# A fourth of the weight splits: low part from an accumulating DMA instead of a VectorE subtraction

## The chip, the cores and the metric

The kernel runs on one core of one Trainium2 chip. The metric is the device time of one execution in microseconds (us); less is better. Two executions of the kernel before are given, and one execution under the hardware profiler, from which all views below come. The engines are TensorE (PE, with its weight loads shown apart as PEld), VectorE (DVE), ScalarE (ACT), GpSimd (POOL) and SyncE (SP), and 16 DMA engines that move data between HBM and the on-chip memory.

## What is computed

A two-layer decoder trunk for 256 tokens of width 2048, in float32. Layer 0 has stick-breaking attention, layer 1 has differential attention over keys and values of its own; each layer ends in a squared-ReLU MLP of width 8192. What matters here is that nearly all the work is products of activations with weight matrices, each of which is read from HBM once:

```python
qkv = (x @ w_qkv)                  # 2048 x 6144
...
h = merge_blocks(o) @ w_o          # 2048 x 2048
x = layer_norm(DEEPNORM_ALPHA * x + h, ...)
h = jax.nn.relu(x @ w_up)          # 2048 x 8192
x = layer_norm(DEEPNORM_ALPHA * x + (h * h) @ w_down, ...)
...                                # layer 1: kv = x @ w_kv (2048 x 4096), q = x @ w_q, o @ w_o, MLP
```

## The kernel before

**Split operands.** TensorE multiplies in a format with fewer significant bits than float32 (fp32r). The kernel therefore writes every operand as a sum of a high and a low part and forms three products, high by high, high by low and low by high, in one accumulator. The function `split` makes the parts: ScalarE copies the source into the narrow format, which gives the high part (line 58), and VectorE subtracts that from the source, which gives the low part (line 61).

**Pieces of weights.** `wchunk` delivers the weights in 768 pieces of 128 partitions by 1024 elements, 512 KB each, in the order in which the matmuls use them: 96 for the queries, keys and values of layer 0, 32 for its output projection, 256 for its MLP, then 96, 32 and 256 for layer 1. In this text piece 388, for instance, is the 388th of them. A piece is loaded into a staging tile `st` (4 buffers; the load is issued by SyncE at line 67), its high part goes to `wh` and its low part to `wl` (7 buffers each). So no more than seven pieces are split at a time, and a piece's high part can be written only when the matmuls of the piece seven before it are done.

**Loops.** `by_token` computes 512 output columns for all tokens (one accumulator for each half of the tokens, 12 matmuls a piece; the first call of a phase takes the pieces in runs of two). `by_column` computes the transposed product (four accumulators, 16 matmuls a piece). `out_proj` and the second half of `mlp` use the activations as weights of TensorE and share each activation tile between two pieces. In `mlp`'s second half, blocks of 24 matmuls use two pieces in turn: the first two accumulators of a half of the tokens take the first piece, the other two the second. All matmuls are recorded at line 148 (function `mm`).

**Between phases.** At the end of `out_proj` and `mlp` the function `residual` adds a finished accumulator to `xs` on VectorE, and `layernorm` normalizes 128 tokens: `mv` and `ve` (lines 132 and 134) on VectorE, the inverse root `rstd` on GpSimd (line 136), the scaling of four slices on VectorE (lines 140 and 141), and then four transposes on TensorE (line 90), split again into `xT` (lines 58 and 61). The next phase begins with `by_token`, which uses the first half of the tokens while the second is still being normalized.

**Order.** The code writes down dependencies only; a scheduler at build time fixes the order of the instructions on each engine. Each engine then works through its own list in that order and waits on semaphores. GpSimd had 20 instructions in all: four initial ones, eight `rstd` and eight `rr`, the same kind of inverse root inside the attention of layer 1 (line 490).

The functions that the change touches follow, with the line numbers of the profile.

Of the kernel before, what the change touches and what calls it, by code (L numbers as in the profile page):

```python
# [10 lines left out]
AF = mybir.ActivationFunctionType  # L11
ALU = mybir.AluOpType
AX = mybir.AxisListType

P = 128
# [12 lines left out]
LAMBDA_INIT = 0.8 - 0.6 * math.exp(-0.3 * 1)  # L28
CH = 1024
RUN = 2  # L30
ST_BUFS = 4
W_BUFS = 7

# [2 lines left out]
def trunk(ctx: ExitStack, tc: tile.TileContext, x, ln_g, ln_b, sb_w_qkv, sb_w_o, kv_w, diff_w_q,  # L36
          diff_lambda, diff_subln_g, diff_w_o, mlp_w_up, mlp_w_down, consts, rope, out):
    nc = tc.nc
# [4 lines left out]
    wp = ctx.enter_context(tc.tile_pool(name="wp", bufs=W_BUFS))  # L43
    ps = ctx.enter_context(tc.tile_pool(name="ps", bufs=1, space=bass.MemoryType.PSUM))

    uid = [0]

    def nm(s):
        uid[0] += 1
# [3 lines left out]
        return ps.tile([P, 512], F32, tag=tag, name=nm(tag), bufs=5 if tag == "acc" else 3)  # L53

    def split(hi, lo, src, hi_engine=None):
        """src (float32) = hi + lo exactly, each with at most 12 significant bits."""
        if hi_engine is None:
            nc.scalar.activation(hi, src, AF.Copy)  # L58
        else:
            hi_engine.tensor_copy(hi, src)  # L60
        nc.vector.tensor_tensor(lo, src, hi.bitcast(F32), op=ALU.subtract)  # L61

    def wchunk(src):
        """A [P, a, b] piece of a weight matrix, a * b = CH, as its two parts."""
        a, b = src.shape[1], src.shape[2]
        st = wp.tile([P, CH], F32, tag="st", bufs=ST_BUFS, name=nm("st"))
        nc.sync.dma_start(st.rearrange("p (a b) -> p a b", a=a), src)
        hi = wp.tile([P, CH], F32R, tag="wh", name=nm("wh"))
        lo = wp.tile([P, CH], F32R, tag="wl", name=nm("wl"))
        split(hi, lo, st)  # L70
        return hi.rearrange("p (a b) -> p a b", a=a), lo.rearrange("p (a b) -> p a b", a=a)

# [1 line left out]
    nc.scalar.preload_act_table_set("natural_log_exp_and_others")  # L74
    xs = base.tile([P, NT, D], F32, name="xs")
    xT = base.tile([P, KT, 2, T], F32R, name="xT")
# [7 lines left out]
    nc.vector.memset(neghalf, -0.5)  # L84

    def transposed(t, j, src):
        """src [P tokens, 512] -> its part of xT."""
        pt = acc("at")
        for i in range(4):
            nc.tensor.transpose(pt[:, i * P:(i + 1) * P], src[:, i * P:(i + 1) * P], ident)  # L90
        hi = xT[:, 4 * j:4 * j + 4, 0, t * P:(t + 1) * P]
        lo = xT[:, 4 * j:4 * j + 4, 1, t * P:(t + 1) * P]
        split(hi, lo, pt.rearrange("p (a b) -> p a b", a=4))
# [6 lines left out]
    background = []  # L100

    def tick():
        """Emit the next step of attention between two chunks of a projection."""
        if background:
            step = background.pop(0)
            if step:
                step()

    def load_gb(layer, i, allocate, after):
        """The norm's weights and biases on all partitions, in four pieces. The loads wait for  # L110
        `after`, so that they take no space before the phase that uses them."""
        pieces = []
        for j in range(4):
            sl = slice(j * 512, (j + 1) * 512)
            g, b = allocate(j)
            for piece, src in ((g, ln_g), (b, ln_b)):
                nc.vector.tensor_copy(piece[:, 0:1], after)
                nc.scalar.dma_start(piece, src[layer, i:i + 1, sl].broadcast_to((P, 512)))
            pieces.append((g, b))
        return pieces  # L120
# [27 lines left out]
        nc.tensor.matmul(o, l, r, start=start, stop=stop)  # L148

    def by_token(w, n0, staggered=False, between=None):  # L150
        """[tokens, 512 columns] of x @ w: one accumulator for each half of the tokens."""
        accs = [acc() for _ in range(NT)]
        run = RUN if staggered else 1
        for c0 in range(0, KT // 2, run):
            chunks = [
                wchunk(w[2 * c * P:(2 * c + 2) * P, n0:n0 + 512].rearrange("(a p) n -> p a n", p=P))
                for c in range(c0, c0 + run)
            ]
            for t in range(NT):
                ts = slice(t * P, (t + 1) * P)  # L160
                if between and c0 == 0 and t == 1:
                    between()
                for c, (wh, wl) in zip(range(c0, c0 + run), chunks):
                    for kk in range(2):
                        k = 2 * c + kk
                        mm(accs[t], xT[:, k, 0, ts], wh[:, kk, :], k == 0, False)
                        mm(accs[t], xT[:, k, 0, ts], wl[:, kk, :], False, False)
                        mm(accs[t], xT[:, k, 1, ts], wh[:, kk, :], False, k == KT - 1)
            tick()
        return accs  # L170

    def by_column(w, n0):
        """(x @ w).T for 512 columns: four accumulators [128 columns, 2, tokens], whose two
        halves are to be added."""
        accs = [acc() for _ in range(4)]
        for c in range(KT // 2):
            wh, wl = wchunk(w[2 * c * P:(2 * c + 2) * P, n0:n0 + 512].rearrange("(a p) n -> p a n", p=P))
            for f in range(4):
                fs = slice(f * P, (f + 1) * P)
                for kk in range(2):  # L180
                    k = 2 * c + kk
                    if k == 0:
                        mm(accs[f], wh[:, kk, fs], xT[:, k, :, :], True, False)
                        mm(accs[f][:, :T], wl[:, kk, fs], xT[:, k, 0, :], False, False)
                    else:
                        mm(accs[f][:, :T], wl[:, kk, fs], xT[:, k, 0, :], False, False)
                        mm(accs[f], wh[:, kk, fs], xT[:, k, :, :], False, k == KT - 1)
            tick()
        return accs

    def folded(pool, psum, scale=1.0):
        """The sum of an accumulator's halves, times scale."""
        b = pool.tile([P, T], F32, tag="evb", bufs=2, name=nm("evb"))
        nc.scalar.activation(b, psum[:, T:], AF.Copy, scale=scale)  # L194
        s = pool.tile([P, T], F32, tag="evs", bufs=2, name=nm("evs"))
        if scale == 1.0:
            nc.vector.tensor_tensor(s, psum[:, :T], b, op=ALU.add)  # L197
        else:
            nc.vector.scalar_tensor_tensor(s, psum[:, :T], scale, b, op0=ALU.mult, op1=ALU.add)
        return s  # L200
# [12 lines left out]
        return vs  # L213

    def gb_pieces(pool):
        """Space for the norm's weights and biases where queries and keys were."""
        return lambda j: [pool.tile([P, 512], F32, tag=tag, bufs=4, name=nm("gb")) for tag in "qk"]

    def out_proj(w, oT, gb_of):
        """x = norm(alpha * x + o @ w)"""  # L220
        stats = new_stats()
        lag = 4
        for nh in range(2):
# [5 lines left out]
            for ks in sets:  # L229
# [5 lines left out]
                else:  # L235
                    chunks = {}
# [69 lines left out]
                    if ks[-1] == FT - 1:  # L306
                        layernorm(t, stats[t], gb, last)

# [1 line left out]
    with tc.tile_pool(name="sb", bufs=1) as pool:  # L310
        oT = pool.tile([P, KT, 2, T], F32R, name="oTa")
        w = sb_w_qkv[0]
# [2 lines left out]
        sps = [pool.tile([P, 2, 512], F32R, name=f"sp{i}") for i in range(2)]  # L315
        aps = [pool.tile([P, 2, 512], F32R, name=f"ap{i}") for i in range(2)]

        # Scores lie as [keys, queries]: [later keys, all queries | earlier keys, all queries].
        # The first P columns (later keys, earlier queries) are masked whole and held at zero.
        live, tris = slice(P, 512), slice(P, P + T)  # L320
        blocks = ((1, slice(0, T)), (0, slice(T, 512)))

        def attend(h, q, k, vs):
            """The steps of one head."""
            i = h % 4
            sh, sl = sps[i % 2][:, 0, :], sps[i % 2][:, 1, :]
            ah, al = aps[i % 2][:, 0, :], aps[i % 2][:, 1, :]
# [66 lines left out]
        out_proj(sb_w_o[0], oT, lambda: load_gb(0, 0, gb_pieces(pool), oT[:, KT - 1, 0, 0:1].bitcast(F32)))  # L394
    mlp(0, False)

# [1 line left out]
    with tc.tile_pool(name="df", bufs=1) as pool:  # L398
        oT = pool.tile([P, KT, 2, T], F32R, name="oTb")
        tri = pool.tile([P, T], F32, name="trib")  # L400
# [32 lines left out]
            nc.vector.tensor_tensor(s[0:32, :], s[0:32, :], r, op=ALU.add)  # L433
            return parts(pool, tag, s)

        # Scores lie as [queries, keys]: [later queries, all keys | earlier queries, earlier keys].
        rows = ((1, slice(0, T)), (0, slice(T, 384)))
        tris = slice(P, P + T)

        def attend2(h, qs, ks, vs):  # L440
            """The steps of one head."""
            wT = pool.tile([P, 2, 384], F32R, tag="wT", bufs=2, name=nm("wT"))
            on = pool.tile([P, 2, T], F32, tag="on", bufs=2, name=nm("on"))
            ex = [pool.tile([P, 384], F32, tag=f"p{c}", bufs=2, name=nm("e")) for c in range(2)]
# [81 lines left out]


def _constants():
    """Masks by position and the rotary tables: they depend on the shapes alone."""
    import numpy as np  # L530

    i = np.arange(P)
    before = i[:, None] < i[None, :]
    neg = np.float32(-1e30)
    strict = np.where(before, np.float32(0), neg)
    causal = np.where(before.T | np.eye(P, dtype=bool), np.float32(0), neg)
    consts = np.concatenate([np.eye(P), before.T, np.ones((P, P)), strict, strict, causal, causal], axis=1).astype(
        np.float32)
    rot = 32
    inv = np.float32(500000.0) ** (-np.arange(0, rot, 2, dtype=np.float32) / np.float32(rot))  # L540
    ang = np.arange(T, dtype=np.float32)[:, None] * inv.astype(np.float32)[None, :]
    cos, sin = np.cos(ang).T, np.sin(ang).T
    rope = np.stack([np.concatenate([cos, cos]), np.concatenate([-sin, sin])], axis=1).astype(np.float32)
    return consts, rope
# [23 lines left out]
```

## Time and profile before

| | |
|---|---|
| two executions | 2241.9 and 2241.95 us, median 2241.93 |
| profiled execution, first to last instruction (span) | 2240.6 us |
| busy in the span: TensorE matmuls | 2212.8 us (99%) |
| VectorE | 1360.5 us (61%) |
| ScalarE | 1026.4 us (46%) |
| GpSimd | 14.4 us (1%) |
| mean granted TensorE clock | 0.997 |
| read from HBM | 413.80 MB |

The profile gives the profiled execution by its span alone; the 1.3 us between the span and the timed executions lie ahead of its first or behind its last instruction. Busy time of an engine is the time in which at least one of its instructions runs. The chain of work that ended last is traced back from the last instruction, at each step to what released it. A wait is put down to what ended it.

### The profile page before, as it was taken

The numbers are of one execution on the slowest core, as the hardware profiler recorded it, in microseconds if no ns is written. First come the engines' busy times: TensorE is split into PE (matmuls) and PEld (weight loads), VectorE is DVE, ScalarE is ACT, GpSimd is POOL, SyncE is SP. The second block draws the span as 40 slices with busy tenths as digits, with TensorE's granted clock in tenths as the row PEclk, the third lists the DMA queues.
The fourth block names the chain that finished last, engine by engine and source line by source line (L and its number), as shares of the span: only waits on it lengthen the run. The fifth ranks groups of instructions, "written<-read, shape, count | busy, mean of one in ns | idle before, by whom it ended". The sixth has DMA issues, their size and how long they took to land.

```text
span 2240.6 us, 29321 instructions
## 1 busy us (share of the span) xinstructions
PE 2212.8 (99%) x11314; PEld 1873.3 (84%) x11314; DVE 1360.5 (61%) x1865; ACT 1026.4 (46%) x1346; POOL 14.4 (1%) x20
## 2 busy tenths in 40 slices
PE   8999999999999999999999999999999999999997
PEld 7888888788888888888878888887888888888886
DVE  5776675755555545544678777657555555455446
ACT  5655553444444444444445555434444444444442
POOL 0000000000000000000000000000000000000000
PEclk9999999999999999999999999999999999999999
DMA  7555556566666666656555555665666666665563
GB/s 263 176 161 170 168 170 221 164 188 188 188 188 188 192 216 202 190 195 196 171 183 162 172 162 183 191 195 179 188 188 188 188 188 192 223 193 192 197 196 104
DMA packets 176637, 417.81 MB, mean 186 GB/s; under 512 B 13137, under 2 KB 13649, under 8 KB 176498
## 3 DMA queue, kind: packets, MB, share of 16 engines
q1 hardware_dynamic: 170544, 405.52, 57.8%
q10 hardware_dynamic: 5954, 10.42, 1.5%
q8 instruction: 88, 1.44, 0.2%
q14 instruction: 51, 0.42, 0.1%
HBM read 413.80 MB, written 2.10 MB: 186 GB/s over the span
## 4 chain that ended last, share of the span: by engine, by line
PE 95%; DVE 3%; DMA 1%; issue 0%; ACT 0%; SPq 0%; POOL 0%; DVEq 0%; ACTq 0%; POOLq 0%
PE acc L148 81%; PE at L148 14%; DVE xs L141 1%; DVE wl L61 1%; DVE xs L140 0%; DVE stats L125 0%; DMA st<-in_sb_w_qkv_dram 0%; PE at L90 0%; DVE xT L61 0%; DVE xs L124 0%; DMA st<-in_mlp_w_up_dram 0%; ACT wh L58 0%; PE at L499 0%; PE at L472 0%; PE at L267 0%
## 5 line engine op out<-in xcount | busy, mean ns | idle before, releaser
L61 DVE TENSOR_TENSOR wl<-st,wh 128x1024 fp32r<-128x1024 f32 x768 | 938.6, 1224 | 823.4 <-ACT wh L58 808.1
L58 ACT ACTIVATE wh<-st 128x1024 fp32r<-128x1024 f32 x768 | 812.2, 1059 | 1044.1 <-PE acc L148 984.5
L148 PE MATMUL acc<-xT,wh 128*128 128x512 f32 x2944 | 1021.4, 393 | 0.3 <-ACT k L58 0.3
L148 PE MATMUL acc<-xT,wl 128*128 128x256 f32 x2944 | 793.6, 280 | 0.0
L148 PEld LDWEIGHTS acc<-xT,wh 128*128 128x128 f32 x2944 | 540.5, 188 | 115.0 <-ACT k L58 0.6
L148 PEld LDWEIGHTS acc<-xT,wl 128*128 128x128 f32 x2944 | 551.6, 187 | 16.3
L148 PE MATMUL acc<-wh,hp 128*128 128x512 f32 x1280 | 414.2, 389 | 0.0
L148 PEld LDWEIGHTS acc<-wh,hp 128*128 128x128 f32 x1280 | 240.3, 188 | 49.9
L148 PE MATMUL at<-wh,hp 128*128 128x512 f32 x768 | 256.7, 389 | 0.0
L148 PE MATMUL acc<-wl,hp 128*128 128x512 f32 x640 | 249.0, 389 | 0.0
L148 PE MATMUL acc<-wh,xT 128*128 128x512 f32 x640 | 212.7, 401 | 2.9 <-ACT wh L58 2.1
L148 PEld LDWEIGHTS at<-wh,hp 128*128 128x128 f32 x768 | 144.1, 188 | 29.8
L148 PE MATMUL at<-wl,hp 128*128 128x512 f32 x384 | 149.4, 389 | 0.0
L148 PEld LDWEIGHTS acc<-wh,xT 128*128 128x128 f32 x640 | 120.1, 189 | 30.8 <-ACT wh L58 2.4
L148 PEld LDWEIGHTS acc<-wl,hp 128*128 128x128 f32 x640 | 120.1, 188 | 25.0
L148 PE MATMUL acc<-wl,xT 128*128 128x512 f32 x320 | 128.1, 400 | 4.9 <-DVE wl L61 4.8
L194 ACT ACTIVATE evb<-acc 128x256 f32<-128x256 f32 x184 | 69.3, 378 | 39.7 <-DVE evs L197 31.9
L148 PEld LDWEIGHTS at<-wl,hp 128*128 128x128 f32 x384 | 72.1, 188 | 15.0
L148 PE MATMUL acc<-wh,oTa 128*128 128x512 f32 x256 | 80.3, 390 | 0.0
L148 PE MATMUL acc<-wh,oTb 128*128 128x512 f32 x256 | 80.2, 391 | 0.0
L148 PEld LDWEIGHTS acc<-wl,xT 128*128 128x128 f32 x320 | 60.6, 189 | 19.2 <-DVE wl L61 6.6
L197 DVE TENSOR_TENSOR evs<-acc,evb 128x256 f32<-128x256 f32 x152 | 60.1, 416 | 0.8
(104 smaller groups left out, 1052.4 us busy)
## 6 DMA issues: line engine op xcount, KB each, us to landing
st<-in_mlp_w_up_dram SPq DMA_DIRECT2D x256, 512.0 KB, 3.6
st<-in_mlp_w_down_dram SPq DMA_DIRECT2D x256, 512.0 KB, 3.9
st<-in_sb_w_qkv_dram SPq DMA_DIRECT2D x96, 512.0 KB, 4.0
st<-in_kv_w_dram SPq DMA_DIRECT2D x64, 512.0 KB, 4.1
st<-in_sb_w_o_dram SPq DMA_DIRECT2D x32, 512.0 KB, 4.0
st<-in_diff_w_q_dram SPq DMA_DIRECT2D x32, 512.0 KB, 3.8
st<-in_diff_w_o_dram SPq DMA_DIRECT2D x32, 512.0 KB, 4.3
gb<-in_ln_g_dram ACTq DMA_DIRECT2D x16, 256.0 KB, 5.4
```

The source lines that it names most:

```text
L58: nc.scalar.activation(hi, src, AF.Copy)
L61: nc.vector.tensor_tensor(lo, src, hi.bitcast(F32), op=ALU.subtract)
L141: nc.vector.scalar_tensor_tensor(y, y, rstd, gb[j][1], op0=ALU.mult, op1=ALU.add)
L148: nc.tensor.matmul(o, l, r, start=start, stop=stop)
L194: nc.scalar.activation(b, psum[:, T:], AF.Copy, scale=scale)
L197: nc.vector.tensor_tensor(s, psum[:, :T], b, op=ALU.add)
```

## The change

A counter numbers the pieces, and for every fourth piece `wchunk` takes another path. ScalarE first writes the negated high part into the low part's tile (a copy with scale -1, rounded like the high part). GpSimd's queue then issues a DMA that reads the same 512 KB of weights from HBM a second time and adds them to what the tile holds, so that weights minus high part remain. ScalarE writes the high part from the staging tile as before. VectorE has nothing to do for such a piece.

```diff
+BY_DMA = 4
...
-    uid = [0]
+    uid, chunk_no = [0], [0]
...
         hi = wp.tile([P, CH], F32R, tag="wh", name=nm("wh"))
         lo = wp.tile([P, CH], F32R, tag="wl", name=nm("wl"))
-        split(hi, lo, st)
+        chunk_no[0] += 1
+        if chunk_no[0] % BY_DMA == 0:
+            nc.scalar.activation(lo, st, AF.Copy, scale=-1.0)
+            nc.gpsimd.dma_start(lo.rearrange("p (a b) -> p a b", a=a), src, accum_op=ALU.add)
+            nc.scalar.activation(hi, st, AF.Copy)
+        else:
+            split(hi, lo, st)
```

The rest of the diff blanks comments. Lines behind the new constant move by 1 (61 becomes 62, 58 becomes 59), and lines behind `wchunk` by 7 (148 becomes 155, 136 becomes 143).

The number of low parts in VectorE's list falls from 768 to 576, ScalarE's list gains 192 copies into `wl`, and GpSimd's list gains 192 DMAs. SyncE's list is the same. The scheduler also moves some instructions. Three places matter below. In the names, the number behind `wh_`, `wl_` or `st_` tells one buffer use from another.

The first place is the start of the program on TensorE, where the first four pieces are multiplied (`acc_119` is the accumulator of the first half of the tokens, `acc_120` that of the second; `wl_194` is the low part of piece 4, and `wh_187`, `wl_188` belong to piece 3). Before:

```order
L148 MATMUL acc_119<-wh_193,xT 128x512
L148 MATMUL acc_119<-wl_194,xT 128x512
L148 MATMUL acc_119<-wh_193,xT 128x512 x2
L148 MATMUL acc_119<-wl_194,xT 128x512
L148 MATMUL acc_119<-wh_193,xT 128x512
L148 MATMUL acc_120<-wh_187,xT 128x512
L148 MATMUL acc_120<-wl_188,xT 128x512
L148 MATMUL acc_120<-wh_187,xT 128x512 x2
L148 MATMUL acc_120<-wl_188,xT 128x512
L148 MATMUL acc_120<-wh_187,xT 128x512
L148 MATMUL acc_120<-wh_193,xT 128x512
```

The same place now:

```order
L155 MATMUL acc_119<-wh_193,xT 128x512
L155 MATMUL acc_120<-wh_187,xT 128x512
L155 MATMUL acc_120<-wl_188,xT 128x512
L155 MATMUL acc_120<-wh_187,xT 128x512 x2
L155 MATMUL acc_120<-wl_188,xT 128x512
L155 MATMUL acc_120<-wh_187,xT 128x512
L155 MATMUL acc_120<-wh_193,xT 128x512
L155 MATMUL acc_119<-wl_194,xT 128x512
L155 MATMUL acc_119<-wh_193,xT 128x512 x2
L155 MATMUL acc_119<-wl_194,xT 128x512
```

Seven matmuls that don't need `wl_194` now stand ahead of its first use.

The second place is ScalarE at the same time, from the high part of piece 3 (`wh_187`) on. Before:

```order
L58 ACTIVATE wh_187<-st_185 128x1024
L58 ACTIVATE xT<-at_159 128x4x128
L58 ACTIVATE wh_193<-st_191 128x1024
L58 ACTIVATE wh_223<-st_221 128x1024
L58 ACTIVATE xT<-at_166 128x4x128
```

Now:

```order
L59 ACTIVATE wh_187<-st_185 128x1024
L59 ACTIVATE xT<-at_159 128x4x128
L75 ACTIVATE wh_193<-st_191 128x1024
L59 ACTIVATE wh_224<-st_222 128x1024
L59 ACTIVATE xT<-at_166 128x4x128
L73 ACTIVATE wl_194<-st_191 128x1024
```

The negated copy for piece 4, on which its DMA waits, stands behind the last transposed slice of the input; the copy of the high part was put ahead of it.

The third place is the end of layer 0's MLP. GpSimd's list there held nothing between the inverse roots. Now, where `rstd_9395` and `rstd_9469` are those of the two halves of the tokens, it reads:

```order
L74 DMA wl_9303<-in_mlp_w_down_dram 128x1024
L74 DMA wl_9355<-in_mlp_w_down_dram 128x1024
L74 DMA wl_9577<-in_kv_w_dram 128x2x512
L143 TENSOR_TENSOR rstd_9395<-ve_9393,neghalf 128x1
L143 TENSOR_TENSOR rstd_9469<-ve_9467,neghalf 128x1
L74 DMA wl_9650<-in_kv_w_dram 128x2x512
```

And on ScalarE, where `wl_9577` and `wh_9576` are the parts of piece 388 and `xT<-at_9399` is the first transposed slice after the norm:

```order
L59 ACTIVATE wh_9570<-st_9568 128x1024
L73 ACTIVATE wl_9577<-st_9574 128x1024
L75 ACTIVATE wh_9576<-st_9574 128x1024
L59 ACTIVATE wh_9607<-st_9605 128x1024
L59 ACTIVATE wh_9613<-st_9611 128x1024
L59 ACTIVATE wh_9643<-st_9641 128x1024
L59 ACTIVATE xT<-at_9399 128x4x128
```

The DMA of piece 388 now stands ahead of the first inverse root on GpSimd, and its copy into `wl_9577` ahead of the first `xT` on ScalarE.

## Prediction

> **What bounds the kernel now.** I read the page's busy line first, then its chain, then the waits of TensorE and of ScalarE.
>
> ```profile
> PE 2212.8 (99%) x11314; PEld 1873.3 (84%) x11314; DVE 1360.5 (61%) x1865; ACT 1026.4 (46%) x1346; POOL 14.4 (1%) x20
> PE 95%; DVE 3%; DMA 1%; issue 0%; ACT 0%; SPq 0%; POOL 0%; DVEq 0%; ACTq 0%; POOLq 0%
> PE acc L148 <- DVE wl L61: 4.8, 3, 2.5
> ACT wh L58 <- PE acc L148: 984.5, 583, 6.4
> 2236.11 1.41 DVE L141 SCALAR_TENSOR_TENSOR xs<-xs,rstd,gb 128x512 f32<-128x512 f32 x2
> ```
>
> TensorE is busy for 99% of the span, and the chain that ended last runs through it for 95%. Of its idle time, 2240.6 - 2212.8 = 27.8 us, most lies at the two ends (it waits for the first input, and the last norm runs behind its last matmul until after 2236). The part that VectorE's subtraction causes is the third row: three waits, 4.8 us together. The fourth row says the rest: ScalarE waited 984.5 us for matmuls to give a buffer back. The split pieces run as far ahead of TensorE as seven buffers allow, so a faster split has nowhere to go. **This is a TensorE-bound kernel, and the change frees VectorE.** The most it can win by that is a few us; the question is what it can lose.
>
> **What is removed.** VectorE gives up 192 of these:
>
> ```profile
> L61 DVE TENSOR_TENSOR wl<-st,wh 128x1024 fp32r<-128x1024 f32 x768 | 938.6, 1224 | 823.4 <-ACT wh L58 808.1
> L58 ACT ACTIVATE wh<-st 128x1024 fp32r<-128x1024 f32 x768 | 812.2, 1059 | 1044.1 <-PE acc L148 984.5
> 411.34 0.50 PE L148 MATMUL acc<-wl,xT 128*128 128x512 f32 x1 [1.19 <-DVE wl L61]
> 1128.85 0.50 PE L148 MATMUL acc<-wl,xT 128*128 128x512 f32 x1 [2.46 <-DVE wl L61]
> 1520.87 0.50 PE L148 MATMUL acc<-wl,xT 128*128 128x512 f32 x1 [1.17 <-DVE wl L61]
> ```
>
> 192 x 1.224 = 235 us of VectorE, nearly all beside running matmuls. On the path are only the last three rows, each after a norm, where VectorE is busy with the second half of the tokens. Each phase begins on a multiple of four pieces (128, 384 and 512 go before), and counting the pieces in program order the waits are for numbers 132, 388 and 516: the fourth of their phase, whose low parts no longer come from VectorE. I take all three off: **-4.8 us**. Behind piece 388, for instance, the next subtraction has one less ahead of it, so nothing of that size takes the place of the wait.
>
> ScalarE gains 192 copies of 1.06 us, 203 us, hidden by its 1044 us idle, except where a list position matters (below).
>
> **What a DMA costs in the steady state.** No row shows an accumulating DMA. The nearest are the plain loads:
>
> ```profile
> q1 hardware_dynamic: 170544, 405.52, 57.8%
> 800.00:1060.00 260.00, 260.00 (x1149) 215.29 (x1148) 131.32 (x124) 114.45 (x120) 0.00 (x0) 1.00 0.62 198
> 1055.29 3.40 PE acc L148 x15
> ...
> 1060.73 3.40 PE acc L148 x15
> DMA to landing us min/median/max: 3.3/3.7/8.6
> ```
>
> The first row is the queue of the loads: 57.8% of 2240.6 us is 1295 us, over 768 pieces 1.69 us of all 16 engines for one. An accumulating transfer moves at least as much: **1.69 us is the lower end**; less is excluded, since the same 512 KB come from HBM. Reading what the tile holds, too, makes two passes, 3.38 us; read, read and write one after the other makes three, 5.07; the upper end is 8.6, the engines held for the whole of the slowest landing in the last row. I take **3.38**, since the two reads are what is added and the write is there in a plain load as well; it is also nearer to the row for a plain load than to the slowest landing.
>
> The second row is a stretch of an MLP's second half: the granted clock is 1.00 and the DMA engines are 0.62 busy. The two rows of the chain give its pace: a block of two pieces takes 1060.73 - 1055.29 = 5.44 us, four pieces 10.88. In that time the engines have to move 4 x 1.69 + 3.38 = 10.14 us of work, 93%. It fits, and **costs 0**. The cover is gone when one accumulation takes over 10.88 - 6.76 = 4.12 us, 2.4 times a plain load.
>
> The Trainium skill, "Collectives: The Full Stack", section "The bandwidth ceiling: the fold count and why AG ≠ RS ≠ AR", says that a reducing DMA is slower than a copy because of its two source reads, not its adder, with 62.28 against 32.35 GB/s. By that ratio an estimate is 1.69 x 1.93 = 3.25 us, 92% of the engines; no row here shows it.
>
> **Its latency in the steady state.** A landing takes 3.7 us by the last row's median; I add 1.7 for the second read and 1 for GpSimd to issue it (its nearest row, an inverse root, is 0.92, quoted below): **6.4 us**. The ends are 3.3 and three of the slowest landings in a row, 25.8. In the MLP's second half piece n may be written when piece n-7 is used up. For the fourth piece of every four, the second of its block, that is three quarters through a block, and its first use comes a quarter into the third block after it: 0.25 + 2 + 0.25 blocks of 5.44, 13.6 us. The negated copy takes 1.06 of it, so 12.5 us are left for a landing of 6.4. It is hidden, with 6 us to spare.
>
> SyncE's loads share the engines, so their landings get later, but their list is unchanged, and `st` was given back by VectorE's subtraction; now it comes back with ScalarE's second copy, 2.1 us after the first begins, where copy and subtraction took 2.3.
>
> **Where the cover is thin: the start.**
>
> ```profile
> 18.56 0.59 ACT L58 ACTIVATE xT<-at 128x512 fp32r<-128x512 f32 x1
> 22.01 0.40 PE L148 MATMUL acc<-wl,xT 128*128 128x512 f32 x1
> 22.72 0.40 PE L148 MATMUL acc<-wl,xT 128*128 128x512 f32 x1
> ```
>
> Piece 4's low part was first used at 22.01. The order puts seven other matmuls ahead; three take 0.71 us by the last two rows, so it is needed at 23.66. The negated copy stands behind the `xT` of the first row, from 19.15 to 20.2; 6.4 later is 26.6. **+2.9 us**, and with the ends of the landing nothing or up to 22. Behind the waiting matmul stand all others on TensorE.
>
> **The boundary at 1116.** GpSimd's list has the DMA of piece 388 ahead of the inverse root, ScalarE's has one more copy ahead of the first `xT`.
>
> ```profile
> 1116.53 0.92 POOL L136 TENSOR_TENSOR rstd<-ve,neghalf 128x1 f32<-128x1 f32 x1 [702.86 <-DVE ve L134]
> 1117.62 1.41 DVE L141 SCALAR_TENSOR_TENSOR xs<-xs,rstd,gb 128x512 f32<-128x512 f32 x2
> 1118.85 1.04 ACT L58 ACTIVATE wh<-st 128x1024 fp32r<-128x1024 f32 x1
> 1119.80 1.07 ACT L58 ACTIVATE xT<-at 128x512 fp32r<-128x512 f32 x2
> 1120.43 0.50 PE L148 MATMUL acc<-wh,xT 128*128 128x512 f32 x1 [0.69 <-ACT xT L58]
> ```
>
> The inverse root had 0.2 us to spare before line 141 (1116.53 + 0.92 against 1117.62); an issue of 1 us in front of it delays VectorE's scaling by 0.8. ScalarE went from copies to `xT` without a pause, so one more copy delays `xT` by 1.06, and TensorE waited for it (last row). The two delays run side by side: **+1.1 us**. Ends: 0 if GpSimd and ScalarE get there earlier, since the copy's buffer may come free sooner; some 8 if GpSimd is held for a slow landing.
>
> **The end.**
>
> ```profile
> 2210.24 1.06 ACT L58 ACTIVATE wh<-st 128x1024 fp32r<-128x1024 f32 x1 [2.50 <-PE acc L148]
> 2217.07 0.39 PE L148 MATMUL at<-wl,hp 128*128 128x512 f32 x1
> ```
>
> The last piece, 768, is a fourth too: copied by 2211.3, used at 2217.07, 5.8 us for a landing of 6.4: **+0.6 us** (nothing to 20).
>
> **Sum.** -4.8 + 0 + 2.9 + 1.1 + 0.6 = -0.2 us on a span of 2240.6: 2240.4, and 1.3 us outside the span as in the runs shown (2241.93): 2241.7. I say **2242 us**, no change. About 2% is what a measurement of this kernel can tell from no change here.
>
> **The rivals.**
>
> *The DMA engines become the bound* (slower). Mechanism: the weights stream at the engines' pace, in every group of four pieces, once an accumulation takes over 4.12 us of them. At three passes (5.07) a group takes 11.83; 192 groups make 2271, and with TensorE's idle time but for the three waits (27.8 - 4.8 = 23) and the 1.3 us outside the span about **2295 us**. At four times a load (6.76) it is 13.52 a group, 2620 in all; at 8.6 it is 2973. For it: the 0.62 in the window, and that no row shows the adder. Against: in the first slices the loads alone ran faster than they need later.
>
> ```profile
> GB/s 263 176 161 170 168 170 221 164 188 188 188 188 188 192 216 202 190 195 196 171 183 162 172 162 183 191 195 179 188 188 188 188 188 192 223 193 192 197 196 104
> ```
>
> 263 GB/s over the first 56 us against 188 in the MLP: the 1.69 us contain waiting, and there is room that the busy share doesn't show.
>
> The Trainium skill, "DMA: Bandwidth & Descriptors", section "Issuing engines are not separate DMA queues", says that DMAs of every issuing engine run on the same 16 DMA engines and interleave. It speaks for this rival: GpSimd's queue brings no bandwidth of its own, and by it the sum is the one above; no row has GpSimd's queue.
>
> *The landing outlasts the lead* (slower). It is decided at 12.5 us. Above that, TensorE waits once in each of the 64 groups of the two MLPs' second halves, where a piece is used longest; at 14 us that is 1.5 x 64 = 96 us, about **2338 us**, and 25.8 would give 851 us. The slowest load, 8.6, is against it. Below 12.5 only the thin places pay: at 9 us the start costs 5.5 and the end 3.2, the sum is +5 and the time 2247; at 12.5 they cost 9.0 and 6.7 and it is 2254, with a few us more where a phase begins.
>
> *The norms gain more than the waits* (a little faster). VectorE's list is a subtraction shorter between the norm's steps at each of the three boundaries: 3 x 1.2 = 3.7 us more, if TensorE had waited for them, and nothing lost at the start: **2235 us**. TensorE's other waits after norms are 0.3 us each, which speaks against it.
>
> *The change doesn't do what it says*: the list shows that VectorE has 576 subtractions left; that is certain. That this frees nothing on the path is the forecast itself.
>
> **Chances and range.** The forecast with its thin places, 2235 to 2256, has 0.70 (0.08 of it the faster rival); 2256 to 2285, a landing or a contention at the edge of the cover, 0.10; the DMA bound 0.15; the lead outlasted 0.05. Faster by over 2% would be under 2197, less than the matmuls' own 2212.8: 0.01, taken out of the forecast's share. Slower by over 2% is over 2287: 0.20. The range 2235 to 2285 holds 8 in 10.
>
> **What would show it.** Right: TensorE busy about 2213 us; VectorE near 1125 and ScalarE near 1230; the three waits on `wl` gone; a wait of some 3 us on a DMA into `wl` before 30 us and almost none later; DMA share in the MLP near 0.9 or lower; landings of `wl` of 5 to 8 us. Wrong: TensorE idle in the MLPs with waits on `st` (the engines are the bound) or on `wl` (the landing outlasts the lead). What would make the prediction wrong is above all the adder's pace, which nothing here shows.

## The result and the profile after

| | before | after |
|---|---|---|
| median | 2241.93 us | 2260.91 us (2257.15 and 2264.67) |
| profiled execution: span | 2240.6 us | 2262.9 us |
| TensorE, VectorE, ScalarE, GpSimd busy | 2212.8, 1360.5, 1026.4, 14.4 us | 2219.6, 1131.7, 1196.4, 218.0 us |

The ratio is 1.0081 (95% interval 1.0062 to 1.01): the change costs 0.8%. That lies inside the range and is no change by the bound of 2%, but it isn't the 2242 us of the forecast: the change costs 19 us by the medians and 22.3 by the two spans. The page of the changed kernel, first the busy line, then two of its DMA queues, then the chain:

```profile
PE 2219.6 (98%) x11314; PEld 1878.3 (83%) x11314; DVE 1131.7 (50%) x1673; ACT 1196.4 (53%) x1538; POOL 218.0 (10%) x212
q1 hardware_dynamic: 170544, 405.52, 55.1%
q0 software_dynamic: 42240, 100.68, 26.0%
PE 91%; DMA 3%; DVE 3%; issue 2%; ACT 1%; POOL 0%; SPq 0%; DVEq 0%; ACTq 0%; POOLq 0%
```

VectorE is 229 us less busy, as forecast, and the end doesn't come sooner. The new queue of GpSimd takes 26.0% of 2262.9 us, 588 us for 192 DMAs: 3.06 us of all 16 engines for one, where a load takes 55.1% / 768, 1.62 us. DMAs now make up 3% of the chain instead of 1%. The next rows are the same window in an MLP's second half as before, and the landings of GpSimd's DMAs and of the loads into `st` (each from its issue, in us):

```profile
800.00:1060.00 260.00, 260.00 (x1148) 215.29 (x1148) 103.17 (x102) 133.34 (x144) 19.78 (x23) 1.00 0.86 248
DMA to landing us min/median/max: 5.5/9.0/11.7
DMA to landing us min/median/max: 3.4/5.3/12.1
```

In the steady state TensorE is busy for 260.00 of 260 us at full clock, as before, with the DMA engines at 0.86 instead of 0.62. The cost isn't there. But a landing takes 9.0 us, not 6.4, and the loads beside them take 5.3 instead of 3.7. The waits of TensorE show where that is late:

```profile
PE acc L155 <- DMA wl<-in_sb_w_qkv_dram: 8.2, 1, 8.2
PE acc L155 <- DMA wl<-in_kv_w_dram: 4.8, 2, 3.7
PE acc L155 <- DMA wl<-in_mlp_w_up_dram: 4.3, 2, 2.5
PE at L97 <- DVE xs L148: 2.1, 5, 0.5
PE acc L155 <- DVE wl L62: 1.4, 2, 1.1
PE acc L155 <- DVE xs L131: 1.1, 1, 1.1
```

Five waits on an accumulating DMA make 17.3 us. They belong to pieces 4, 136, 392, 396 and 520, all within the first twelve pieces of a phase; in the rest of the run there is none. The waits on VectorE's subtractions fell from 4.8 to 1.4 us, but those on the norm's slices (`xs`, line 148, two more of them) rose from 0.9 to 2.1. Below are four of the waiting matmuls, and the windows behind the waits of pieces 136, 4, 396 and 520 (the third number from the end of a row is the granted clock):

```profile
32.82 0.76 PE L155 MATMUL acc<-wl,xT 128*128 128x512 f32 x1 [8.21 <-DMA wl<-in_sb_w_qkv_dram]
440.98 0.47 PE L155 MATMUL acc<-wl,xT 128*128 128x512 f32 x1 [2.50 <-DMA wl<-in_mlp_w_up_dram]
1176.25 0.36 PE L155 MATMUL acc<-xT,wl 128*128 128x256 f32 x1 [3.69 <-DMA wl<-in_kv_w_dram]
1558.58 0.47 PE L155 MATMUL acc<-wl,xT 128*128 128x512 f32 x1 [1.81 <-DMA wl<-in_mlp_w_up_dram]
441.00:445.00 4.00, 4.00 (x17) 3.21 (x18) 1.25 (x2) 2.61 (x3) 0.00 (x0) 1.00 1.04 309
32.00:38.00 6.00, 5.18 (x14) 4.16 (x15) 1.23 (x1) 1.67 (x2) 0.00 (x0) 0.58 1.07 298
1176.00:1180.00 4.00, 3.75 (x14) 3.31 (x15) 2.17 (x2) 2.12 (x2) 0.00 (x0) 0.63 0.85 209
1559.00:1563.00 4.00, 4.00 (x12) 3.10 (x11) 1.23 (x1) 1.54 (x2) 0.00 (x0) 0.57 1.08 341
```

Behind three of the four waits TensorE goes on at half its clock: 12 matmuls in 4 us at 1559, clock 0.57, against 17 in 4 us at 441, clock 1.00. By the trace's clock records the half clock lasts for 10.24 us around piece 4 (4.2 of them behind the wait) and for 3.41 us each behind the waits of 396 and 520. At half clock the matmuls behind the wait of piece 4 follow each other every 0.43 us, later every 0.23, so about half of that time is lost: 2.1, 1.7 and 1.7 us.

When the last matmul of each piece ends in the two traces tells where the 22.3 us arose:

| place | shift, us | made of |
|---|---|---|
| ahead of piece 4 | +0.8 | the first matmuls begin later |
| piece 4 | +10.4 | wait 8.2, half clock 2.1 |
| 132 and 133, 517 | -1.2, -1.2 | the waits on VectorE that are gone |
| 136 | +2.5 | wait |
| 385 to 394 | +0.5 | the wait of 2.46 at 388 gives way to 1.06 at 389; 392 waits 1.1; the norm's slices are later |
| 396 | +5.5 | wait 3.7, half clock 1.7 |
| 415 to 426, 497 | +0.5, +1.3 | short waits on VectorE |
| 519, 520 | +3.4 | wait 1.8, half clock 1.7 |

From piece 5 to the norm behind 128, from 137 to 384 and from 521 to the end the shift stays within 0.3 us; between 415 and 496 it swings by about 1 us.

### The profile page after: what moved, and what is told of

Its sections match the earlier page's. It is cut to its first block, busy times and chain, and to the rows that moved or that the text cites. A ratio compares the mean times of both kernels' runs of the same rounds, so it can differ in the third digit from the quotient of the medians.

```text
span 2262.9 us, 29765 instructions
## 1 busy us (share of the span) xinstructions
PE 2219.6 (98%) x11314; PEld 1878.3 (83%) x11314; DVE 1131.7 (50%) x1673; ACT 1196.4 (53%) x1538; POOL 218.0 (10%) x212
## 3 DMA queue, kind: packets, MB, share of 16 engines
q1 hardware_dynamic: 170544, 405.52, 55.1%
## 4 chain that ended last, share of the span: by engine, by line
PE 91%; DMA 3%; DVE 3%; issue 2%; ACT 1%; POOL 0%; SPq 0%; DVEq 0%; ACTq 0%; POOLq 0%
PE acc L155 77%; PE at L155 14%; DMA st<-in_diff_w_o_dram 1%; DMA wl<-in_mlp_w_up_dram 1%; DVE wl L62 1%; DVE xs L148 1%; DVE xs L147 1%; DMA wl<-in_sb_w_qkv_dram 1%; DMA wl<-in_kv_w_dram 0%; DVE stats L132 0%; DVE xs L131 0%; DMA st<-in_sb_w_qkv_dram 0%; ACT wh L59 0%; DMA st<-in_kv_w_dram 0%; DVE xT L62 0%
## 5 line engine op out<-in xcount | busy, mean ns | idle before, releaser
L62 DVE TENSOR_TENSOR wl<-st,wh 128x1024 fp32r<-128x1024 f32 x576 | 704.5, 1224 | 1036.0 <-ACT wh L59 1028.9
L73 ACT ACTIVATE wl<-st 128x1024 fp32r<-128x1024 f32 x192 | 203.5, 1060 | 300.5 <-PE acc L155 266.8
L74 POOL DMA_DIRECT2D wl<-in_mlp_w_up_dram x64 | 77.1, 1205 | 608.0 <-ACT wl L73 337.6
L74 POOL DMA_DIRECT2D wl<-in_mlp_w_down_dram x64 | 55.1, 861 | 643.7 <-ACT wl L73 643.7
```

Source lines behind the costliest of these rows:

```text
L73: nc.scalar.activation(lo, st, AF.Copy, scale=-1.0)
L74: nc.gpsimd.dma_start(lo.rearrange("p (a b) -> p a b", a=a), src, accum_op=ALU.add)
```

## The experiments

The theory is that only landings at thin places cost time, and with them the clock behind the waits. The rival is that the second stream of weights slows the loads and the rest everywhere, and the thin places are where it shows.

**The six thin pieces back on VectorE.** Pieces 4, 136, 392, 396, 520 and 768 take the subtraction; 186 DMAs remain.

```diff
-        if chunk_no[0] % BY_DMA == 0:
+        if chunk_no[0] % BY_DMA == 0 and chunk_no[0] not in THIN:
```

> Pieces 4, 136, 392, 396, 520 and 768 get their low part from VectorE again, the other 186 fourths by the DMA. Theory (late landings): the whole loss of 19 us sits in these six places, where the lead is shorter than copy plus landing (about 10.3 us), with the TensorE clock that drops after the waits; the steady state is free. Then 2239 to 2242 us, no wait of TensorE on a DMA into wl, no drop of the clock in mid-kernel. Rival (contention): the 26% that the DMAs add to the DMA engines make loads late everywhere; then about 186/192 of the loss stays, 2255 to 2261 us.

Measured: 2242.82 us against 2243.08 before, ratio 1.000 (0.9991 to 1.0009). With 97% of the added traffic still there, the whole loss is gone. The stream itself costs nothing in the steady state, so the rival falls there. What is left of waits on DMAs is at piece 8, and one at piece 128 of 0.33 us; another wait stands at piece 497, on `residual` (line 132, which is line 131 before this edit). The section on the prediction comes back to it, since there the stream does delay the loads:

```profile
q0 software_dynamic: 40736, 97.53, 25.5%
35.15 0.50 PE L156 MATMUL acc<-wl,xT 128*128 128x512 f32 x1 [1.49 <-DMA wl<-in_sb_w_qkv_dram]
1472.88 0.50 PE L156 MATMUL acc<-wh,oTb 128*128 128x512 f32 x1 [1.42 <-DVE xs L132]
```

**Only the six thin pieces by DMA**, all others by VectorE.

```diff
-        if chunk_no[0] % BY_DMA == 0:
+        if chunk_no[0] in THIN:
```

> The other way round: pieces 4, 136, 392, 396, 520 and 768 alone by the DMA, 762 by VectorE. Theory (late landings): most of the loss is here with 6 of 192 DMAs; the landings are a little shorter as there is less traffic (8 instead of 9 us), so 2252 to 2260 us. Rival (contention): six DMAs add nothing to the traffic, 2242 to 2244 us.

Measured: 2269.12 us, ratio 1.0121 (1.0107 to 1.0135), above what was expected. Six DMAs cost 26 us, more than 192: VectorE's waits behind the norms are back, the DMA waits are no shorter, and in this trace the half clock follows five waits (pieces 4, 136, 388, 392, 520) instead of three:

```profile
PE acc L156 <- DMA wl<-in_mlp_w_up_dram: 7.2, 2, 3.8
PE acc L156 <- DMA wl<-in_sb_w_qkv_dram: 7.1, 1, 7.1
PE acc L156 <- DVE wl L63: 5.2, 4, 2.5
PE acc L156 <- DMA wl<-in_kv_w_dram: 2.8, 1, 2.8
DMA to landing us min/median/max: 5.6/9.4/10.4
```

The last row is those six alone, at 9.4 us: late landings need no neighbours of their own kind. The 5.6 is piece 768, at the end, where few loads are left.

**No DMA at all.** The negated copy is written and the DMA left out.

```diff
             nc.scalar.activation(lo, st, AF.Copy, scale=-1.0)
-            nc.gpsimd.dma_start(lo.rearrange("p (a b) -> p a b", a=a), src, accum_op=ALU.add)
```

> Every fourth piece gets the negated copy, but the accumulating DMA is left out, so that its low part is minus the high part. VectorE and ScalarE are as in the change. It shows what VectorE's relief alone is worth. Theory: the waits on VectorE's subtraction after the three norms go (-1.2, -2.5, -1.2 us), 2236 to 2240 us. Rival (VectorE's relief is worth nothing, or ScalarE's copies cost as much): 2241 to 2244 us.

Measured: 2238.2 us, ratio 0.998 (0.9971 to 0.9989). This is all that VectorE's relief on every fourth piece is worth: 4.9 us by the medians, 3.5 by the two profiled spans (2240.6 and 2237.1).

**Every second piece by DMA** (`BY_DMA = 2`, 384 DMAs).

> Every second piece by the DMA (384 instead of 192). By the busy shares of the changed kernel a load takes 1.62 us of the 16 engines (55.1% of 2262.9 over 768) and an accumulation 3.06 (26.0% over 192). Four pieces then need 6.5 + 6.1 = 12.6 us in the MLPs against TensorE's 10.88. If the busy share is the bound: about 2440 us, and TensorE waits in the MLPs' middle. If the share contains waiting and the engines have room (rival): the steady state stays free, and only more pieces at the starts of phases are late, 2265 to 2285 us.

Measured: 2285.42 us, ratio 1.0192 (1.0176 to 1.0207). The window in the MLP and the queue:

```profile
800.00:1060.00 260.00, 260.00 (x1149) 215.29 (x1148) 75.67 (x78) 155.19 (x168) 41.31 (x48) 1.00 1.04 297
q0 software_dynamic: 84480, 201.35, 48.6%
```

The DMA engines' share is 1.04, with 297 GB/s, and TensorE is still busy for all of the 260 us. A share of 1 was no bound in this window. Much of the +41 us is again at phases' beginnings: +7.1 by the end of piece 2 (1.5 of it at piece 1 already), +9 at the pieces around 128 to 130, +4.3 at 384 to 387. Pieces 401 and 402 add 5.6 in another way: ScalarE waits 1.5 and 2.4 us for loads into `st`, its copies and VectorE's steps behind them come late, and TensorE waits 3.3 us in all for VectorE's `evs`, with a half clock of 3.41 us. So outside the MLPs twice as many DMAs do make loads late enough to cost time.

**The same DMAs without the addition.** What makes a landing 9 us long? Here the DMA overwrites the negated copy, so the low part is the weights themselves.

```diff
-            nc.gpsimd.dma_start(lo.rearrange("p (a b) -> p a b", a=a), src, accum_op=ALU.add)
+            nc.gpsimd.dma_start(lo.rearrange("p (a b) -> p a b", a=a), src)
```

> The change with the addition taken out of the DMA: GpSimd's queue loads the same 512 KB into the low part's tile instead of adding them to what it holds. The low part is then the weights themselves, so the output is not the reference's. What makes a landing take 9.0 us (median, from the issue) where the loads of SyncE's queue took 5.3? Theory A, the addition (a second read of the tile): landings of the low parts fall to 5 to 6 us, packets of 2 KB from 178 ns to about 85, the queue's share from 26.0% to about 14%, the waits at pieces 4, 136, 396 and 520 shrink by 3 us each, and the time is 2247 to 2252. Theory B, the way a DMA of GpSimd's queue is put together (its first packet moves 2.3 us after the issue): packets fall to about 85 ns, but landings stay at 8 to 9 us, the waits stay, and the time is 2257 to 2262.

Measured: 2247.27 us, ratio 1.002 (1.0011 to 1.0029). The queue's share, the landings, and the two waits of TensorE on a DMA into `wl` that are left:

```profile
q0 software_dynamic: 42240, 100.68, 16.8%
DMA to landing us min/median/max: 3.9/7.2/9.3
PE acc L155 <- DMA wl<-in_sb_w_qkv_dram: 4.6, 1, 4.6
PE acc L155 <- DMA wl<-in_mlp_w_up_dram: 1.7, 1, 1.7
```

Neither theory alone: the landing falls by 1.8 us, to 7.2, where SyncE's loads of the MLP's first half take 4.4 in the same run. So of the 4.6 us by which an accumulation (9.0) lands later than those, 1.8 go with the addition and 2.8 stay with GpSimd's queue. The first packet moves 1.4 us after the issue (median), with the addition 2.3. The engines' time for one is 16.8% of 2246.9 / 192, 1.97 us, against 3.06 with the addition. These 1.8 us and the shorter issue were worth 13.6 us of time (2260.91 - 2247.27), since 6.3 us of waits on DMAs into `wl` remain of 17.3: at the edge of a lead a little latency decides on a wait and on the clock behind it.

**Only pieces 132, 388 and 516 by DMA**, the three whose low parts TensorE waited for before. The edit is shown against the run with only the six.

```diff
-THIN = (4, 136, 392, 396, 520, 768)
+THIN = (132, 388, 516)
```

> Only pieces 132, 388 and 516, whose low parts TensorE waited for behind a norm (1.19, 2.46 and 1.17 us), take the DMA; all others keep VectorE's subtraction. Theory: these three have 12 to 14 us for copy and landing, which take about 10.3, so nothing is late and the waits of 132 and 516 go; that of 388 goes in part, since its DMA stands ahead of the inverse root. Ratio 0.998 to 0.999 (2238 to 2240), near the 2238.2 with no DMA at all. Rival: a lone DMA lands later than its lead, or its wait turns the clock to half, as with the six DMAs alone (2269.1): then 2245 or more, with waits on a DMA into wl at these pieces.

Measured: 2238.97 us against 2242.69, ratio 0.9985 (0.9976 to 0.9994). **Faster than both kernels**, with three DMAs. They land in time, at no more than 7.6 us, and one wait on VectorE's subtraction is left, 1.05 us:

```profile
DMA to landing us min/median/max: 7.2/7.3/7.6
PE acc L156 <- DVE wl L63: 1.1, 1, 1.1
PE at L98 <- DVE xs L149: 2.1, 5, 0.6
```

The last row shows what comes next at the norms: 1.2 us more of short waits for their slices than before, as in the change.

**Piece 4 by DMA, and twelve in the middle of layer 0's MLP**: every sixteenth of pieces 160 to 240 in rows of 2 KB and of pieces 272 to 352 in rows of 4 KB.

> Piece 4 by DMA, and beside it every sixteenth piece in the middle of layer 0's MLP (six of its first half in rows of 2 KB, six of its second half in rows of 4 KB), all others by VectorE. Theory: only piece 4 costs something, 10 to 11 us: a wait of 7 to 8 us on its landing and about 2 us more because the granted clock is half of full for some 10 us behind it; time 2252 to 2254. The twelve in the MLP cost nothing. If the rows of the DMA set the landing, the six of 128 rows land about 3 us sooner than the six of 256; if the loads beside them do, both take about 9 us. Rival for the cost at piece 4: the late DMA delays the next pieces' loads or copies, so that more waits follow behind piece 8 and the cost is above 12 us without a change of the clock.

Measured: 2253.85 us, ratio 1.0051 (1.0035 to 1.0066). Piece 4 alone shifts everything behind it by 9.8 us (from -0.4 ahead of it to +9.4), its wait of 7.66 and 2.1 of half clock. The twelve cost nothing, and the rival with further waits falls: behind it the shift stays between 9.2 and 9.8, but for a few matmuls at piece 388 (10.2). Rows of 4 KB don't help:

```profile
wl<-in_mlp_w_up_dram POOLq DMA_DIRECT2D x6, 512.0 KB, 8.4
wl<-in_mlp_w_down_dram POOLq DMA_DIRECT2D x6, 512.0 KB, 8.7
```

Half the rows make GpSimd's issue shorter (0.86 against 1.2 us), not the landing. What shares the engines with it fits better: the last piece, with few loads beside it, took 5.6 with six DMAs in all.

**The same, with 36 matmuls by zeros ahead of the waiting one.** The lines that make the tile of zeros are left out here.

```diff
+                        if chunk_no[0] == 4 and (t, c, kk) == (0, 3, 0):
+                            for _ in range(FILL):
+                                mm(accs[t], zeros, wh[:, kk, :], False, False)
                         mm(accs[t], xT[:, k, 0, ts], wl[:, kk, :], False, False)
```

> As the kernel with piece 4 and twelve pieces of the MLP by DMA, but 36 matmuls with a tile of zeros as weights stand ahead of the one that waits for piece 4's low part; they add zero to the accumulator and keep TensorE busy for about 8 us. Theory (the idle time halves the clock): the wait shrinks to under 2 us, no half clock behind it, and although the landing is no sooner the kernel is about 2 to 3 us faster than without them, 2250 to 2251. Rival (the half clock has another cause, such as the start or the load of the DMA engines): the half clock between 26 and 37 us stays, the 36 matmuls take up to 16 us, and the time is the same or up to 8 us longer.

Measured: 2252.87 us, ratio 1.0046 (1.0032 to 1.006), 1 us below the kernel without them; the intervals overlap. The windows of piece 4, first without the filling, then with it:

```profile
26.00:32.00 6.00, 0.93 (x2) 0.83 (x3) 2.45 (x2) 2.76 (x3) 0.00 (x0) 0.70 1.07 315
32.00:38.00 6.00, 6.00 (x21) 4.71 (x20) 2.45 (x2) 1.47 (x2) 0.00 (x0) 0.73 0.69 226
```

```profile
26.00:32.00 6.00, 5.97 (x26) 4.48 (x24) 1.66 (x3) 2.12 (x2) 0.00 (x0) 1.00 1.05 284
32.00:38.00 6.00, 5.53 (x24) 4.51 (x25) 2.46 (x3) 2.12 (x2) 0.00 (x0) 1.00 0.63 227
32.47 0.47 PE L159 MATMUL acc<-wl,xT 128*128 128x512 f32 x1 [0.50 <-DMA wl<-in_sb_w_qkv_dram]
```

The clock stays at 1.00 and the DMA share is as high: the half clock comes from TensorE's idle time. The half clock of piece 4 cost 2.1 us, but the expected gain of 2 to 3 us did not come, because the seven matmuls that had stood ahead of the wait now stand behind it, about 1.6 us at 24 matmuls in 5.44 us, and the program's start was later in this run (1.4 us at piece 1, where the other had -0.4).

**Two pieces behind each norm by DMA** (131 and 132, 387 and 388, 515 and 516).

> Two pieces behind each norm (131 and 132, 387 and 388, 515 and 516) by DMA, all others by VectorE, where the run with one behind each norm (132, 388, 516) took 2238.97 and left a wait of 1.05 us on VectorE at 388. Theory: taking a second subtraction off VectorE's list there removes that wait, 1 us at most: 2237.5 to 2239. Rival: two DMAs in a row land later than one (7.3 us apart from each other at worst, since GpSimd issues them one after the other and they share the engines with the loads), and the waits come back as waits on a DMA into wl: 2241 to 2246, ratio 1 or above.

Measured: 2239.09 us, ratio 0.9982 (0.9973 to 0.9991): the same as with one. The rival didn't occur (no wait on a DMA into `wl`), but a wait of 1.05 us on VectorE's subtraction stayed too. It had been put down to the wrong piece: by the order of the matmuls it is 389's, the next in VectorE's list behind the two, and to take 387 away, which is split before the norm, could not help it.

**Piece 389 too**: 132, 388, 389 and 516 by DMA.

> Pieces 132, 388, 389 and 516 by DMA. With 132, 388 and 516 alone (2238.97 us) and with 131, 387 and 515 as well (2239.09) one wait of 1.05 us on VectorE was left behind the norm at 1116. Its matmul begins at 1128.81, and by the use of the pieces' low parts in the trace that is piece 389, the subtraction that comes next in VectorE's list. Theory: VectorE's list there holds the norm of the second half of the tokens, and each piece taken off it only passes the wait on to the next one unless that one has time enough; the low part of 390 was ready 1.7 us behind that of 389 and needed 1.7 us behind it, so with 389 gone 390 is early enough. The wait goes: 2237.5 to 2238.5, ratio 0.9975 to 0.9985. Rival: the wait is passed on, to 390 by VectorE or to 389 as a wait on its DMA, which is issued second and has 11.5 us from copy to use for a copy and landing of 9 to 10: wait of 0.5 to 1.5 us, 2238.5 to 2240.

Measured: 2237.41 us against 2242.86, ratio 0.9975 (0.9966 to 0.9985), **the fastest of all**, 5.4 us below the kernel before. TensorE's waits on VectorE behind the norms, and the four landings:

```profile
PE at L98 <- DVE xs L149: 1.6, 4, 0.6
PE acc L156 <- DVE xT L63: 0.5, 1, 0.5
PE acc L156 <- DVE wl L63: 0.5, 2, 0.3
DMA to landing us min/median/max: 7.1/7.6/9.7
```

The wait of 1.05 is gone. The 9.7 is piece 389, whose DMA is issued second: it landed 0.04 us before its use, so there is no room for a third.

**Every fourth piece but for thirteen with short leads** (4, 8, 128, 136, 384, 388, 392, 396, 496, 500, 512, 520 and 768 on VectorE).

> Every fourth piece by DMA but for thirteen that have less than about 13 us between their copy and their first use or stand near a norm (4, 8, 128, 136, 384, 388, 392, 396, 496, 500, 512, 520, 768), which keep VectorE's subtraction. 179 DMAs remain. Theory: nothing is late, so the time is that of the kernel before with the waits of 132 and 516 gone and that of 388 still there: 2239 to 2241, ratio 0.998 to 1.000; the 176 DMAs in the steady state bring nothing over the three behind the norms (2238.97). Rival (freeing VectorE and ScalarE's buffers in the steady state is worth something once nothing is late): under 2238, ratio below 0.998.

Measured: 2240.47 us, ratio 0.9991 (0.9983 to 1.0). As the theory has it: no wait on a DMA into `wl`, the waits of 132 and 516 gone, that of 388 (2.5 us) back. 179 DMAs give no more than three.

## Why the prediction was right and wrong

The time lies in the band of 2256 to 2285 us that had a chance of 0.10, "a landing or a contention at the edge of the cover", and not in the 2235 to 2256 that had 0.70. Two of the signs named for a right forecast failed with it: landings of 5 to 8 us (9.0), and one wait of some 3 us on a DMA with almost none later (8.2, and four later).

**What bounds the kernel, and the steady state: right.** TensorE stays fully busy in the MLPs. The accumulation was taken at 3.38 us of the engines and measured 3.06, 1.89 times the 1.62 of a load. The Trainium skill's ratio of 1.93 ("Collectives: The Full Stack", section "The bandwidth ceiling: the fold count and why AG ≠ RS ≠ AR") agrees with that 1.89. The lead in the MLP's second half, reckoned as 13.6 us from block times, is 13.1 to 13.9 in the trace.

**The rival of the DMA engines as the bound: wrong in its condition.** It was to decide at a full share of the engines. The run with 384 DMAs had a share of 1.04 in the window and TensorE was not held up; so the share says little on how much more would fit. What is left of this rival is late loads between the MLPs, at pieces 401 and 402 in that run and at 497 in the change.

**The landing: the mis-sized term.** 6.4 us was 3.7 + 1.7 + 1: a load, a second read, an issue. Measured 9.0, and 10.3 with the copy ahead of it (median). The runs split it into the 4.4 of a load beside plain DMAs of that queue, 2.8 for GpSimd's queue and 1.8 for the addition. In the MLP's second half 2.5 us were to spare at the least and 3.5 as a median, not 6.

**The list of thin places: the step that failed.** The prediction named the start, piece 388 and piece 768, and said that below 12.5 us "only the thin places pay": 2247 us at a landing of 9. It had the lead from the steady state and looked for thin places only at the start, a norm and the end; the "few us more where a phase begins" stand there for a landing of 12.5 alone and without a price. A phase begins with pieces that are copied late and used soon: by the trace piece 136 has 7.8 us from the beginning of its copy to the matmul that needs it, 520 has 7.8, 396 has 9.6. A copy and a landing take 10.3 as a median, 10.2 and 9.5 at 136 and 520; at 396 they took 13.2 (its landing 11.3), so most of its wait of 3.7 comes from a slow landing: with 10.3 it would have been 0.7. 136, 396 and 520 cost 2.5, 5.5 and 3.4 us with their half clocks, 11.4 in all; that they were missing is half of the error of 22 us, and piece 4 is 7.5 of the rest (10.4 against 2.9).

**The start: sign right, size wrong.** +2.9 us were forecast for piece 4, or 5.5 at a landing of 9; it was +10.4. There the landing took 11.5 us from the issue (the engines' share there is 1.07), and 2.1 us came from the clock, which the sum had not at all.

**The clock: left out.** The prediction held TensorE's clock for constant. It lost 5.5 us of the 22 (2.1 + 1.7 + 1.7), contained in the figures of pieces 4, 396 and 520.

**The gain: right in kind, not whole.** -4.8 us were taken off for three waits; the run without DMAs gained 4.9. That the two agree is in part luck, since in its trace a wait of 1.05 us at piece 389 is left and its span is only 3.5 us shorter. The change got 1.2 and 1.2 at 132 and 516. At 388 the step "nothing of that size takes the place of the wait" failed: piece 389, the next subtraction, waited 1.06 us, and the norm's slices and piece 392 took back the rest. The boundary, forecast as -2.5 + 1.1, came out at +0.5. The run with 389 by DMA too shows that the wait was only passed on. **The end**, forecast at +0.6, cost nothing: piece 768 landed in 5.5 us.

**Piece 497: late loads, in neither the sum nor the theory.** Ahead of it the weights of the norm (`gb`) are loaded beside the pieces. Three loads into `st` issued at 1466 to 1471 us landed 10.3 to 12.1 us later; in the kernel before, two at the same place took 6.7 and 6.4. ScalarE waited for them, so a subtraction came late on VectorE, `residual` (line 131 now, 124 before) stood behind it, and TensorE waited for its accumulator. The first three rows are of the changed kernel, the last of the one before:

```profile
1480.44 1.06 ACT L59 ACTIVATE wh<-st 128x1024 fp32r<-128x1024 f32 x1 [2.55 <-DMA st<-in_diff_w_o_dram]
1486.24 1.23 DVE L62 TENSOR_TENSOR wl<-st,wh 128x1024 fp32r<-128x1024 f32 x1 [3.48 <-ACT wh L59]
1487.38 0.68 DVE L131 SCALAR_TENSOR_TENSOR xs<-xs,acc 128x512 f32<-128x512 f32 x1
1467.52 0.69 DVE L124 SCALAR_TENSOR_TENSOR xs<-xs,acc 128x512 f32<-128x512 f32 x1 [1.08 <-PE acc L148]
```

With 496, 500 and 512 on VectorE two loads there took 8.5 and 7.6 us and TensorE did not wait. So the rival of the second stream holds here, for 1.3 of the 22 us.

## What to carry to other kernels

Freeing an engine that isn't the bound is worth the waits that it ends, and these can be counted in the waits of the bound engine (three, 4.8 us): move only those pieces and the ones that the wait is passed on to (2237.41 us with 4 DMAs, 2260.91 with 192). A replacement with a longer latency has to be checked against the lead of every phase's first pieces, not against the steady state alone. And a wait of the bound engine can cost more than its length, since the clock behind it may be half.

## What the hardware showed that was not expected

- A wait of TensorE in the middle of the run can be followed by half a clock, in units of 3.41 us: after waits of 8.2, 7.7, 3.7 and 1.8 us, not after the one of 2.5 at piece 136, nor after one of 3.0 at piece 128 in the run with 384 DMAs. A wait of 2.46 us on VectorE at piece 388 was followed by it in three kernels (with the six alone, with piece 4 and twelve more, and with thirteen left out), and not in two (the one before and the filled one). The clock of two such windows is 0.67 and 1.00:

```profile
1126.00:1130.00 4.00, 3.25 (x9) 2.58 (x10) 4.00 (x7) 0.00 (x0) 0.00 (x0) 0.67 0.49 133
```

```profile
1128.00:1132.00 4.00, 3.09 (x12) 2.25 (x13) 4.00 (x7) 0.00 (x0) 0.02 (x1) 1.00 0.46 135
```

The first row is of the kernel with every fourth piece but thirteen by DMA, the second of the kernel before. The Trainium skill, "TensorE: Matmul & The Clock Gate", section "What's actually happening", describes a window of 3413 ns that runs freely and a half clock after an idle one. The units of 3.41 us agree; that 1.8 us of idle time can be enough is shorter than the whole idle window that it names. In each trace all changes of the clock lie on one grid of 3.41 us, and what differs is how much of a wait falls into one unit of it. The unit ahead of the half clock was idle for 76% at 396, 53% at 520 and 72% in the first row; the two units that the wait at 136 falls on were idle for 38% and 35%, those of the second row for 43% and 31%. In all thirteen traces a unit at full clock that was idle for over 55% was followed by half a clock, one idle for under 48% never; between the two both occur.

- An accumulating DMA of 512 KB lands 9.0 us after its issue, a plain one from the same queue 7.2, a load from SyncE's queue 4.4 to 5.3 beside them; alone at the end the accumulation takes 5.6.
- The DMA engines' busy share can be 1.04 over 260 us while TensorE waits for nothing.
